# Attention steps traced one at a time between the projections' matmuls, with TensorE held to that order

## The chip, the core and the metric

One core of a Trainium2 chip runs the whole program. The metric is the device time of one execution in microseconds. The engines that matter are TensorE (PE in the rows; its weight loads are listed apart as PEld), VectorE (DVE), ScalarE (ACT) and GpSimd (POOL). They run side by side and wait for one another through semaphores. Matmuls write to PSUM, which has eight banks of 128x512 floats.

## The reference

The program is a two-layer encoder trunk over 256 tokens of width 2048, in float32. Every layer norms its input, projects it, runs attention heads of width 128, multiplies the heads' outputs with a SiLU gate, projects back and adds the residual.

```python
# layer 0
proj = rms_norm(h) @ w_in_even              # q,k,v of A; q,k,v of B; gate
ya = gqa_attention(qa, ka, va)              # 8 heads, q and k normed and rotated
p  = softmax(s1) - lam * softmax(s2)        # 8 differential heads, ALiBi bias
yb = rms_norm(p @ vb, b_subln_g, 1e-5) * (1 - lambda_init)
h  = h + (concat(ya, yb) * silu(gate)) @ w_out_even
# layer 1
yc = 16 heads, softmax(scores + ALiBi + log(window count)) @ vc
h  = h + (yc * silu(gate)) @ w_out_odd
out = rms_norm(h)
```

## The kernel before

**Jobs.** All projections run as jobs. A job (`job_t`, L163) makes 512 output columns for both token tiles (t = 0, 1; 128 tokens each) in two PSUM banks of the pool `acc` (four banks). Its 2048 input channels are 16 steps k. Each float32 product is three single-pass matmuls on float32r halves (`mm3`, L157): high by high, high by low, low by high, at L159, L160 and L161. So a job is 96 matmuls whose weights (the stationary side) are 128 channels by 128 tokens of the activations and whose moving side is 512 columns of the projection matrix. `wgroup` (L135) loads the matrix in pieces of 512 KB, ScalarE rounds each to its high half (L151) and VectorE subtracts to get the low half (L152); both have the planner's high priority. There are 13 jobs of 512 columns for the even input projection, 4 for the even output, 16 for the odd input, and 3 of 512 columns with two of 256 for the odd output.

**Attention.** Results leave a job token-major (tokens on partitions): `evac_t`, `gate_t`, `evac_v` (L212 to L278) scale and copy them. `turned` (L228) transposes a pair of heads, four transposes of 128x128 through TensorE into a bank of the pool `att` (four banks, shared by all of attention). Then each head has six matmuls of 256 columns for its scores (eight for a differential head: four for each of its two softmaxes), a softmax on VectorE and ScalarE, four transposes of the weights p (`transposed`, L312), a split into halves `ph` and `pl`, and the weighted values: six matmuls of 256 columns with v as the stationary side, so the head's output comes out head-major (128 head channels on partitions, 256 tokens along the row), as the output projection wants it.

**A differential head** (`head_b`, L375) needs a norm along the head channels, which lie on partitions. It copies its output out of PSUM (L383), transposes it back to tokens (L388, two), squares and sums, makes the reciprocal root on GpSimd, spreads that over partitions by two more transposes of a broadcast column (L392), and multiplies with the gate, which `pair_gate` (L243) has turned head-major by four transposes for each pair.

**Order.** The program is traced job by job, and whole groups of heads between jobs, but the Tile planner places the instructions. It plays the program on its own timeline and lets each engine take the ready instruction of the highest priority. So TensorE's order is the planner's, and the attention of one group lies among the matmuls of the jobs after it. Each engine then runs its list strictly in that order.

The layer boundary matters too: the output projection of layer 0 (L526) reads `y`, the gated outputs of all 16 heads, and its first job is traced after the last differential head.

Of the kernel before, what the change touches and what calls it, by code (L numbers as in the profile page):

```python
# [17 lines left out]
P = 128  # L18
D = 2048
S = 256  # L20
# [73 lines left out]
def trunk(ctx, tc, x, xt, w_even, w_oe, w_odd, w_oo, gain_cols, rows, final_g, rope_c, geo_c, out):  # L94
# [16 lines left out]
    V, A, G, T = nc.vector, nc.scalar, nc.gpsimd, nc.tensor  # L111
# [45 lines left out]
    def mm3(ps, ah, al, bh, bl, start, stop):  # L157
# [5 lines left out]
    def job_t(w, c0, wd, a, beside=None, pieces=lambda kg: 1):  # L163

        kn = 1024 // wd
        ps = [acc.tile([P, 512], F32, tag="acc", name=f"acc_t{t}")[:, :wd] for t in range(NT)]
        for kg in range(NK // kn):
            hi, lo = wgroup(w, c0, wd, kg, pieces=pieces(kg), beside=beside)
            for t in range(NT):
                for kk in range(kn):  # L170
                    k = kg * kn + kk
                    ts = slice(t * P, (t + 1) * P)
                    mm3(ps[t], a[k][:, 0, ts], a[k][:, 1, ts], hi[:, kk], lo[:, kk], k == 0, k == NK - 1)
        return ps

# [3 lines left out]
    u = [ug[k // UG][:, k % UG] for k in range(NK)]  # L179

    def make_u(k, src, gain):

        A.activation(u[k][:, 0], src, AF.Copy, scale=gain)  # L183
        V.scalar_tensor_tensor(u[k][:, 1], src, gain, f(u[k][:, 0]), op0=ALU.mult, op1=ALU.subtract)
# [43 lines left out]
    def turned(z, pair):  # L228

        ps = att.tile([P, 512], F32, tag="att", name="zt")  # L230
        for j in range(2):
            for t in range(NT):
                c = (2 * pair + j) * HD
                T.transpose(ps[:, j * S + t * P:j * S + (t + 1) * P], z[:, t, c:c + HD], ident)  # L234
        return ps.rearrange("p (j k) -> p j k", j=2)

    def pair_t(z, pair, tag, bufs=2):
        ps = turned(z, pair)
# [4 lines left out]
    def pair_gate(z, pair):  # L243
        ps = turned(z, pair)
        gt = heads.tile([P, 2, S], F32, tag="gate", name="gate", bufs=3)
        A.copy(gt, ps)
        return gt
# [3 lines left out]
    def pair_q64(z, pair):  # L251
        ps = turned(z, pair)
        t = heads.tile([P, 2, 2, S], F32R, tag="q", name="q", bufs=2)
        for j in range(2):
            js, other = slice(64 * j, 64 * j + 64), slice(64 - 64 * j, 128 - 64 * j)
            A.activation(t[js, :, j], ps[js], AF.Copy)
            V.tensor_sub(t[other, :, j], ps[js], f(t[js, :, j]))
        return t

    def pair_k64(z, pair):  # L260
        ps = turned(z, pair)
# [22 lines left out]
    y = [None] * NK  # L284

# [26 lines left out]
    def transposed(p, ps):  # L312
        for kt in range(NT):
            for t in range(NT):
                T.transpose(ps[:, kt * S + t * P:kt * S + (t + 1) * P], p[:, t, kt * P:(kt + 1) * P], ident)  # L315
        ph = heads.tile([P, NT, S], F32R, tag="ph", name="ph")
        pl = heads.tile([P, NT, S], F32R, tag="pl", name="pl")
        pv = ps.rearrange("p (t k) -> p t k", t=NT)
        split(ph, pl, pv)
        return ph, pl  # L320

# [6 lines left out]
    def weighted_v(h, p, v, vs, gate, ps):  # L328
        ph, pl = transposed(p, ps)
        o = ps[:, :S]  # L330
        for kt in range(NT):
            mm3(o, v[:, kt, 0, vs], v[:, kt, 1, vs], ph[:, kt], pl[:, kt], kt == 0, kt == NT - 1)
        finish_y(h, o, gate)

    def head_a(h, q, k, v, vs, gate):
        ps = bank()
        sp = scores(ps, q[:, 0], q[:, 1], k[:, 0], k[:, 1])
# [4 lines left out]
        weighted_v(h, p, v, vs, gate, ps)  # L342
# [13 lines left out]
    def softmax_b(i, q, kh, kl):  # L356
        bias = alibi(2.0 ** -(i + 1), False)
        es, rd = [], []
        for j in range(2):
# [7 lines left out]
            es.append(s)  # L367
        V.tensor_scalar_mul(rd[1], rd[1], nlam[:, 0:1])
# [4 lines left out]
        return p  # L373

    def head_b(h, p, v, vs, gate):  # L375
        ps = [bank(), bank()]
        ph, pl = transposed(p, ps[0])
        o = ps[1][:, :S]
        for kt in range(NT):
# [5 lines left out]
        ot, rb = ps[0][:, :S], ps[0][:, S:]  # L385
        for t in range(NT):
            ts = slice(t * P, (t + 1) * P)
            T.transpose(ot[:, ts], on[:, ts], ident)  # L388
            square_sum(ss[:, t:t + 1], ot[:, ts])
        r = rsqrt_mean(ss, HD, SUBLN_EPS, NT, "rb")  # L390
        for t in range(NT):
            T.transpose(rb[:, t * P:(t + 1) * P], r[:, t:t + 1].to_broadcast([P, P]), ident)  # L392
        V.scalar_tensor_tensor(on, on, gsub[:, 0:1], gate, op0=ALU.mult, op1=ALU.mult)
        finish_y(h, rb, on)

    def softmax_c(h, q, k):
        bias = alibi(float(np.exp2(np.float32(-8.0 * (h + 1) / 16))), True)
        sp = scores(bank(), q[:, 0], q[:, 1], k[:, 0], k[:, 1])
        p = biased(sp, bias)
# [3 lines left out]
        return p  # L403
# [92 lines left out]
    k_a = pair_t(tok_heads(ps_kv, 1, 2), 0, "ka", 1)  # L496
    for g in range(2):
        c = 512 * g
        zq = tok_heads(job_t(w_even, c, 512, u) if g else ps_q0, 0, 4)
        zg = gate_t(job_t(w_even, GATE_E + c, 512, u), rh)  # L500
        for pair in range(2):
            q = pair_t(zq, pair, "q")
            gate = pair_gate(zg, pair)
            for j in range(2):
                head_a(4 * g + 2 * pair + j, q[:, j], k_a[:, g], v_a[:, 0], slice(g * HD, g * HD + HD), gate[:, j])
        zg = gate_t(job_t(w_even, GATE_E + 1024 + c, 512, u), rh)
        zq = evac_t(job_t(w_even, B_Q0 + c, 512, u), rs)
        zk = evac_t(job_t(w_even, B_K0 + c, 512, u), rstd)
        v = v_tile()
        ps = []  # L510
        for pair in range(2):
            q = pair_q64(zq, pair)
            kh, kl = pair_k64(zk, pair)
            ps += [softmax_b(4 * g + 2 * pair + j, q[:, j], kh[:, j], kl[:, j]) for j in range(2)]
        evac_v(v, job_t(w_even, B_V0 + c, 512, u), rstd)
        for pair in range(2):
            gate = pair_gate(zg, pair)
            for j in range(2):
                head_b(8 + 4 * g + 2 * pair + j, ps[2 * pair + j], v[:, pair], slice(j * HD, j * HD + HD), gate[:, j])


    y_even = list(y)
    un = [acts.tile([P, UG, 2, S], F32R, tag="u", name="u", bufs=NK // UG) for _ in range(NK // UG)]
    u = [un[k // UG][:, k % UG] for k in range(NK)]
    parts_o = small.tile([P, NT, 4], F32, tag="parts4", name="parts4", bufs=1)
    for i, (c0, wd) in enumerate(CHUNKS_E):  # L526
        ps = job_t(w_oe, c0, wd, y_even)
        cs = slice(c0, c0 + wd)
        for t in range(NT):
            V.tensor_add(tok[:, t, cs], tok[:, t, cs], ps[t])  # L530
        for k in range(c0 // P, (c0 + wd) // P):
            ps = att.tile([P, 512], F32, tag="att", name="xps")
            for t in range(NT):
                T.transpose(ps[:, t * P:(t + 1) * P], tok[:, t, k * P:(k + 1) * P], ident)
            make_u(k, ps[:, :S], gcol[:, NK + k:NK + k + 1])
        for t in range(NT):
            square_sum(parts_o[:, t, i:i + 1], tok[:, t, cs])


    for g in range(4):  # L540
# [5 lines left out]
        zq = evac_t(job_t(w_odd, c, 512, u), rs)  # L546
        zk = evac_t(job_t(w_odd, D + c, 512, u), rstd)
        p = []
        for pair in range(2):
            q = pair_t(zq, pair, "q")  # L550
            k = pair_t(zk, pair, "k")
            p += [softmax_c(4 * g + 2 * pair + j, q[:, j], k[:, j]) for j in range(2)]
        v = v_tile()
        evac_v(v, job_t(w_odd, 2 * D + c, 512, u), rstd)
        for pair in range(2):
            gate = pair_gate(zg, pair)
            for j in range(2):
                weighted_v(4 * g + 2 * pair + j, p[2 * pair + j], v[:, pair], slice(j * HD, j * HD + HD), gate[:, j], bank())
# [17 lines left out]
    for i, (c0, wd) in enumerate(CHUNKS[:4]):  # L576
        ps = job_t(w_oo, c0, wd, y)
        for t in range(NT):
            final_add(i, t, slice(c0, c0 + wd), ps[t])

    wl = [acts.tile([P, UG, 2, S], F32R, tag="u", name="u", bufs=NK // UG) for _ in range(NK // UG)]
# [58 lines left out]
```

## Time and profile before

| | us |
|---|---|
| median of 3 runs (919.47 to 920.02) | 919.69 |
| the profiled execution | 919.56 |
| its span, first to last instruction | 917.8 |
| TensorE busy | 907.0 |
| VectorE busy | 559.6 |
| ScalarE busy | 532.6 |
| GpSimd busy | 78.2 |

The profiled execution is 0.13 us under the median, and 1.8 us of it lie outside the span. TensorE's granted clock was 0.998 of its full 2.4 GHz over the span. A matmul's recorded time is longer than its share of the engine, because one starts while the one before drains: what an instruction costs TensorE is read from the distance between two starts, not from its own length.

### The profile page before, as it was taken

To read this page: it belongs to the slowest core of one execution; us is meant where nothing else is said; L and a number is where in the kernel's file an instruction comes from. 1 tells how busy PE (TensorE), PEld (TensorE's weight loads), DVE (VectorE), ACT (ScalarE), POOL (GpSimd) and SP (SyncE) were. 2 spreads that over 40 slices of the span, in tenths; PEclk is the share of its full clock that TensorE was granted. 3 is DMA by queue.
4 is the path that set the end of the run, shared out by engine and by line. 5 is a ranking of instruction groups with operands and counts; after the bars stand their busy time and mean duration, and the time that the engine had idled before them with its cause. 6 is when DMAs were issued, how large, how long until landed. Compare 5 with 4: busy or idle time off the path is not lost.

```text
span 917.8 us, 11973 instructions
## 1 busy us (share of the span) xinstructions
PE 907.0 (99%) x4440; PEld 760.4 (83%) x4440; DVE 559.6 (61%) x751; ACT 532.6 (58%) x866; POOL 78.2 (9%) x67
## 2 busy tenths in 40 slices
PE   9999999999999999999999999999999999999996
PEld 7888888888888887888888888888888888888886
DVE  6685644875766686655544765467445754476563
ACT  7657645875576696555544755456544844474451
POOL 0010000110100012000000400032001300040000
PEclk9999999999999999999999999999999999999999
DMA  8855455354544443455555445543554455555552
GB/s 329 311 211 160 154 189 184 138 189 161 179 160 160 171 151 116 169 198 183 184 201 189 154 144 192 196 162 138 186 194 170 147 174 193 193 170 179 194 196 92
DMA packets 47035, 164.39 MB, mean 179 GB/s; under 512 B 5376, under 2 KB 6144, under 8 KB 46976
## 3 DMA queue, kind: packets, MB, share of 16 engines
q1 hardware_dynamic: 46656, 162.57, 50.7%
q0 software_dynamic: 320, 1.05, 0.5%
q8 instruction: 35, 0.57, 0.3%
q14 instruction: 24, 0.20, 0.1%
HBM read 161.50 MB, written 2.10 MB: 178 GB/s over the span
## 4 chain that ended last, share of the span: by engine, by line
PE 96%; ACT 1%; issue 1%; DMA 1%; SPq 0%; DVE 0%; POOLq 0%; POOL 0%; DVEq 0%; ACTq 0%
PE acc_t L160 29%; PE acc_t L161 29%; PE acc_t L159 29%; PE zt L234 2%; PE bank L315 1%; PE bank L159 1%; PE bank L161 1%; PE bank L160 1%; DMA raw<-in_w_in_even 1%; PE bank L294 1%; PE bank L295 1%; PE bank L293 1%; ACT hi L151 0%; PE bank L363 0%; PE bank L364 0%
## 5 line engine op out<-in xcount | busy, mean ns | idle before, releaser
L152 DVE TENSOR_TENSOR lo<-raw,hi 128x1024 fp32r<-128x1024 f32 (+1 forms) x294 | 359.3, 1223 | 284.1 <-ACT hi L151 283.8
L151 ACT ACTIVATE hi<-raw 128x1024 fp32r<-128x1024 f32 (+1 forms) x294 | 309.4, 1054 | 307.7 <-PE acc_t L161 292.0
L160 PE MATMUL acc_t<-lo,u 128*128 128x512 f32 x928 | 364.9, 395 | 0.1
L161 PE MATMUL acc_t<-hi,u 128*128 128x512 f32 x928 | 362.2, 392 | 0.0
L159 PE MATMUL acc_t<-hi,u 128*128 128x512 f32 x928 | 338.4, 393 | 0.4 <-ACT u L183 0.4
L160 PEld LDWEIGHTS acc_t<-lo,u 128*128 128x128 f32 x928 | 174.6, 188 | 36.2 <-DVE lo L152 0.6
L159 PEld LDWEIGHTS acc_t<-hi,u 128*128 128x128 f32 x928 | 174.0, 188 | 36.1 <-ACT u L183 1.2
L161 PEld LDWEIGHTS acc_t<-hi,u 128*128 128x128 f32 x928 | 174.5, 188 | 33.9
L160 PE MATMUL acc_t<-lo,y 128*128 128x512 f32 (+1 forms) x256 | 96.5, 379 | 0.0
L161 PE MATMUL acc_t<-hi,y 128*128 128x512 f32 (+1 forms) x256 | 95.4, 377 | 0.0
L159 PE MATMUL acc_t<-hi,y 128*128 128x512 f32 (+1 forms) x256 | 90.4, 381 | 0.7 <-ACT hi L151 0.6
L351 POOL TENSOR_SCALAR bias<-geo 128x512 f32<-128x512 f32 x24 | 37.5, 1562 | 572.8 <-DVE s L346 534.3
L160 PEld LDWEIGHTS acc_t<-lo,y 128*128 128x128 f32 x256 | 48.3, 189 | 8.6
L159 PEld LDWEIGHTS acc_t<-hi,y 128*128 128x128 f32 x256 | 47.6, 188 | 9.4 <-ACT hi L151 1.4
L161 PEld LDWEIGHTS acc_t<-hi,y 128*128 128x128 f32 x256 | 48.2, 188 | 8.3
L304 ACT ACTIVATE s<-s,nm 128x256 f32<-128x256 f32 x64 | 31.7, 497 | 4.4 <-DVE nm L301 4.3
L216 ACT ACTIVATE z<-acc_t,rstd 128x512 f32<-128x512 f32 x40 | 27.2, 680 | 9.0 <-PE acc_t L161 9.0
L234 PE MATMUL zt<-ident,z 128*128 128x128 f32 x180 | 29.7, 272 | 0.0
L234 PEld LDWEIGHTS zt<-ident,z 128*128 128x128 f32 x180 | 22.4, 140 | 5.0
L346 DVE TENSOR_TENSOR s<-bank,bias 128x512 f32<-128x512 f32 x32 | 21.7, 682 | 6.9 <-POOL bias L353 4.4
L353 POOL TENSOR_TENSOR bias<-bias,geo 128x512 f32<-128x512 f32 x16 | 23.8, 1490 | 1.3
L210 DVE TENSOR_TENSOR pl<-bank,ph 128x512 fp32r<-128x512 f32 x32 | 21.4, 682 | 2.3 <-ACT ph L209 2.2
(137 smaller groups left out, 696.3 us busy)
## 6 DMA issues: line engine op xcount, KB each, us to landing
raw<-in_w_in_odd SPq DMA_DIRECT2D x128, 512.0 KB, 3.2
raw<-in_w_in_even SPq DMA_DIRECT2D x102, 512.0 KB, 3.3
raw<-in_w_out_even SPq DMA_DIRECT2D x32, 512.0 KB, 3.2
raw<-in_w_out_odd SPq DMA_DIRECT2D x32, 512.0 KB, 3.2
tok<-in_x SPq DMA_DIRECT2D x4, 512.0 KB, 8.8
xk<-in_xt SPq DMA_DIRECT2D x6, 256.0 KB, 6.7
raw<-in_w_in_even SPq DMA_DIRECT2D x4, 256.0 KB, 4.0
gf<-in_final_norm_g POOLq DMA_DIRECT2D x4, 256.0 KB, 4.7
```

Source lines behind the costliest of these rows:

```text
L151: A.activation(hi[:, ks], rv[:, ks], AF.Copy)
L152: splits.append(V.tensor_sub(lo[:, ks], rv[:, ks], f(hi[:, ks])))
L159: T.matmul(ps, ah, bh, start=start, stop=False)
L160: T.matmul(ps, ah, bl, start=False, stop=False)
L161: T.matmul(ps, al, bh, start=False, stop=stop)
L210: V.tensor_sub(lo, src, f(hi))
L216: A.activation(z[:, t], ps[t], AF.Copy, scale=r[:, t:t + 1])
L234: T.transpose(ps[:, j * S + t * P:j * S + (t + 1) * P], z[:, t, c:c + HD], ident)
L304: A.activation(e[:, t], s[:, t], AF.Exp, bias=nm[:, t:t + 1], accum_out=den[:, t:t + 1])
L346: V.tensor_add(s, sp, bias)
L351: G.tensor_scalar_mul(b, geo[:, 0], -slope)
L353: G.tensor_add(b, b, geo[:, 1])
```

## The change

The diff has three parts.

1. **One order for TensorE.** A class `T` replaces `nc.tensor`. Each matmul or transpose is traced with `issue_after` the last one, so TensorE runs them exactly as traced.
2. **A tick list.** Attention becomes generators (tasks). `mm3` of a job calls `tick()` after each of its matmuls; a tick runs one step of one due task, and the task names the number of ticks until its next step. A transpose is a step of its own, the six or twelve matmuls of a head are one step. Waiting times are written as ticks: 36, 46 or 40 from scores to the transposes of the weights, 16 from those to the weighted values, 80 from the evacuation of the A queries to their transposes. The output projections (`jobs_out`) interleave their first two jobs: channels of heads 0 to 11 for both, then those of heads 12 to 15 for both.
3. **Token-major differential heads.** The weighted values take `ph` and `pl` as the stationary side and 128 columns of v as the moving side, twelve matmuls in place of six. The output comes out with tokens on partitions, so norm, gain and gate are applied there; two transposes then turn the gated result. The copy at L383, the transposes at L388 and L392 and the gate's transposes for these heads are gone.

```diff
+    class T:
+        last = None
+        @classmethod
+        def queue(cls, op, *args, **kwargs):
+            with tc.issue_after(cls.last) if cls.last else nullcontext():
+                cls.last = op(*args, **kwargs).ins
...
+    def tick():
+        now[0] += 1
+        for task in list(tasks):
+            if task[0] <= now[0]:
+                try:
+                    wait = next(task[1])
...
+                if wait:
+                    task[0] = now[0] + wait
+                    break
...
         T.matmul(ps, ah, bh, start=start, stop=False)
+        tick()
         T.matmul(ps, ah, bl, start=False, stop=False)
+        tick()
         T.matmul(ps, al, bh, start=False, stop=stop)
+        tick()
...
+    def jobs_out(w, chunks, a):
+        (c0, wd), (c1, _) = chunks[:2]
+        ps = [job_banks(wd) for _ in range(2)]
+        for kgs in (range(6), range(6, 8)):
+            for p, c in zip(ps, (c0, c1)):
+                job_steps(p, w, c, wd, a, kgs)
...
     def turned(z, pair):
...
                 T.transpose(ps[:, j * S + t * P:j * S + (t + 1) * P], z[:, t, c:c + HD], ident)
+                yield 1
...
+    def weights_t(p):
+        n = order[0]
+        order[0] += 1
+        yield from until(("parts", n - 2)) if n > 1 else ()
+        ps = bank()
+        for kt in range(NT):
+            for t in range(NT):
+                T.transpose(ps[:, kt * S + t * P:kt * S + (t + 1) * P], p[:, t, kt * P:(kt + 1) * P], ident)
+                yield 1
...
+        split(ph, pl, ps.rearrange("p (t k) -> p t k", t=NT))
+        yield 16
...
-    def head_b(h, p, v, vs, gate):
-        ps = [bank(), bank()]
-        ph, pl = transposed(p, ps[0])
-        o = ps[1][:, :S]
-        for kt in range(NT):
-            mm3(o, v[:, kt, 0, vs], v[:, kt, 1, vs], ph[:, kt], pl[:, kt], kt == 0, kt == NT - 1)
-        on = work.tile([P, S], F32, tag="on", name="on")
-        A.copy(on, o)
...
-            T.transpose(ot[:, ts], on[:, ts], ident)
...
-            T.transpose(rb[:, t * P:(t + 1) * P], r[:, t:t + 1].to_broadcast([P, P]), ident)
...
+        yield 46
+        ph, pl, used = yield from weights_t(p)
+        yield from until(("v", h))
+        v, vs = values[h]
+        zg, gc = gates[h]
+        o = bank()[:, :S]
+        for t in range(NT):
+            for kt in range(NT):
+                ts = slice(t * P, (t + 1) * P)
+                mm3(o[:, ts], ph[:, kt, ts], pl[:, kt, ts], v[:, kt, 0, vs], v[:, kt, 1, vs], t == kt == 0,
+                    t == kt == NT - 1)
...
+            V.scalar_tensor_tensor(yt[:, ts], o[:, ts], r[:, t:t + 1], zg[:, t, gc], op0=ALU.mult, op1=ALU.mult)
+        yield 18
+        ps = bank()[:, :S]
+        for t in range(NT):
+            ts = slice(t * P, (t + 1) * P)
+            T.transpose(ps[:, ts], yt[:, ts], ident)
+            yield 1
...
         zq = tok_heads(job_t(w_even, c, 512, u) if g else ps_q0, 0, 4)
+        spawn(task_a(g, zq), 80)
...
         zk = evac_t(job_t(w_even, B_K0 + c, 512, u), rstd)
+        spawn(task_bk(g, zk, qs), 14)
```

## Rows read from the trace of the kernel before

**Rows 1.** The page: busy time and share of engines, clock, chain that ended last.
```profile
PE 907.0 (99%) x4440; PEld 760.4 (83%) x4440; DVE 559.6 (61%) x751; ACT 532.6 (58%) x866; POOL 78.2 (9%) x67
...
PEclk9999999999999999999999999999999999999999
...
PE 96%; ACT 1%; issue 1%; DMA 1%; SPq 0%; DVE 0%; POOLq 0%; POOL 0%; DVEq 0%; ACTq 0%
```
**Rows 2.** TensorE's groups: line, tiles, shapes, count; busy us, mean ns; idle before.
```profile
L160 PE MATMUL acc_t<-lo,u 128*128 128x512 f32 x928 | 364.9, 395 | 0.1
...
L234 PE MATMUL zt<-ident,z 128*128 128x128 f32 x180 | 29.7, 272 | 0.0
...
L159 PE MATMUL bank<-ph,v 128*128 128x256 f32 x48 | 13.6, 283 | 0.2 <-ACT ph L209 0.2
...
L388 PE MATMUL bank<-ident,on 128*128 128x128 f32 x16 | 4.4, 280 | 0.3 <-ACT on L383 0.3
```
**Rows 3.** TensorE in order of time, 77 to 83 us: start, length, instruction.
```profile
77.32 0.39 PE L159 MATMUL acc_t<-hi,u 128*128 128x512 f32 x1
...
78.68 0.39 PE L160 MATMUL acc_t<-lo,u 128*128 128x512 f32 x1
78.91 0.27 PE L234 MATMUL zt<-ident,z 128*128 128x128 f32 x1
78.94 0.47 PE L161 MATMUL acc_t<-hi,u 128*128 128x512 f32 x1
79.25 0.63 PE L159 MATMUL acc_t<-hi,u 128*128 128x512 f32 x2
...
81.69 0.28 PE L294 MATMUL bank<-ka,q 128*128 128x256 f32 x1
81.81 0.28 PE L295 MATMUL bank<-ka,q 128*128 128x256 f32 x1
81.93 0.60 PE L234 MATMUL zt<-ident,z 128*128 128x128 f32 x4
...
82.60 0.40 PE L160 MATMUL acc_t<-lo,u 128*128 128x512 f32 x1
```
**Rows 4.** TensorE in order of time at the layer boundary, 347 to 350 us.
```profile
347.06 0.60 PE L315 MATMUL bank<-ident,s 128*128 128x128 f32 x4
348.26 0.73 PE L159 MATMUL acc_t<-hi,y 128*128 128x512 f32 x2 [0.59 <-ACT hi L151]
...
349.41 0.28 PE L159 MATMUL bank<-ph,v 128*128 128x256 f32 x1
350.04 0.33 PE L388 MATMUL bank<-ident,on 128*128 128x128 f32 x1 [0.34 <-ACT on L383]
```
**Rows 5.** Busy us and counts of each engine in 340 to 362 us.
```profile
340.00:362.00 22.00, 20.77 (x110) 16.68 (x109) 16.91 (x34) 15.68 (x42) 6.53 (x5) 1.00 0.44 148
```
**Rows 6.** Weight loads (PEld) at 348 us: start, time covered, count.
```profile
348.25 0.30 PEld L159 LDWEIGHTS acc_t<-hi,y 128*128 128x128 f32 x2 [0.83 <-ACT hi L151]
348.60 0.19 PEld L160 LDWEIGHTS bank<-pl,v 128*128 128x128 f32 x1
```
**Rows 7.** A 256-column matmul whose weights could not be loaded ahead.
```profile
355.25 0.38 PE L159 MATMUL bank<-ph,v 128*128 128x256 f32 x1 [0.17 <-ACT ph L209]
```
**Rows 8.** The first score matmul of the first differential head.
```profile
160.47 0.28 PE L363 MATMUL bank<-kh,q 128*128 128x256 f32 x1
```
**Rows 9.** VectorE, the end of the same head's softmax.
```profile
175.07 0.86 DVE L372 SCALAR_TENSOR_TENSOR s<-s,rden 128x256 f32<-128x256 f32 x2
```
**Rows 10.** VectorE, the low half of transposed weights, those of 343.74 us.
```profile
347.57 0.68 DVE L210 TENSOR_TENSOR pl<-bank,ph 128x512 fp32r<-128x512 f32 x1
```
**Rows 11.** TensorE, those four transposes, 343 to 344 us.
```profile
343.74 0.60 PE L315 MATMUL bank<-ident,s 128*128 128x128 f32 x4
```
**Rows 12.** TensorE, the first projection matmuls after the start, two merged.
```profile
5.27 1.20 PE L159 MATMUL acc_t<-hi,u 128*128 128x512 f32 x2
```

**Rows 13.** TensorE, the last matmul.
```profile
909.52 0.28 PE L161 MATMUL acc_l<-u,y 128*128 128x256 f32 x1
```

More of the change, by code (lines that the diff above doesn't have):

```diff
@@ L155, in wgroup, with spawn, until, advance @@
         return hi, lo
-    def mm3(ps, ah, al, bh, bl, start, stop):
+    tasks, now, done = [], [0], set()
+    def spawn(steps, delay=1):
+        tasks.append([now[0] + delay, steps])
+    def tick():
[4 more added lines that the diff above has]
+                    wait = next(task[1])
+                except StopIteration:
+                    tasks.remove(task)
+                    wait = 1
+                if wait:
+                    task[0] = now[0] + wait
+                    break
+    def until(key):
+        while key not in done:
+            yield 0
+    def advance(finished):
+        while not finished():
+            assert tasks
+            now[0] += 1
+            for task in list(tasks):
+                if task[0] <= now[0]:
+                    try:
+                        task[0] = now[0] + next(task[1])
+                    except StopIteration:
+                        tasks.remove(task)
+    def mm3(ps, ah, al, bh, bl, start, stop, tick=lambda: None):
         T.matmul(ps, ah, bh, start=start, stop=False)
+        tick()
         T.matmul(ps, ah, bl, start=False, stop=False)
+        tick()
         T.matmul(ps, al, bh, start=False, stop=stop)
-    def job_t(w, c0, wd, a, beside=None, pieces=lambda kg: 1):
+        tick()
+    def job_banks(wd):
+        return [acc.tile([P, 512], F32, tag="acc", name=f"acc_t{t}")[:, :wd] for t in range(NT)]
+    def job_steps(ps, w, c0, wd, a, kgs, beside=None, pieces=lambda kg: 1):
         kn = 1024 // wd
-        ps = [acc.tile([P, 512], F32, tag="acc", name=f"acc_t{t}")[:, :wd] for t in range(NT)]
-        for kg in range(NK // kn):
+        for kg in kgs:
             hi, lo = wgroup(w, c0, wd, kg, pieces=pieces(kg), beside=beside)
@@ L241, in pair_t, with pair_gates @@
         return dst
[L243 to L247, printed above, removed]
+    def pair_gates(z, key):
+        for pair in range(2):
+            ps = yield from turned(z, pair)
+            gt = heads.tile([P, 2, S], F32, tag="gate", name="gate", bufs=3)
+            A.copy(gt, ps)
+            for j in range(2):
+                gates[key + 2 * pair + j] = gt[:, j]
+                done.add(("gate", key + 2 * pair + j))
     def pair_q64(z, pair):
-        ps = turned(z, pair)
+        ps = yield from turned(z, pair)
         t = heads.tile([P, 2, 2, S], F32R, tag="q", name="q", bufs=2)
@@ L260, in pair_k64 @@
     def pair_k64(z, pair):
-        ps = turned(z, pair)
+        ps = yield from turned(z, pair)
         kh = heads.tile([P, 2, 2, S], F32R, tag="k", name="kh", bufs=2)
@@ L284, in trunk @@
     y = [None] * NK
+    gates, values, order = {}, {}, [0]
     def bank():
@@ L326, in finish_y, with weighted_v, head_a @@
         split(y[h][:, 0], y[h][:, 1], yf)
-    def weighted_v(h, p, v, vs, gate, ps):
-        ph, pl = transposed(p, ps)
-        o = ps[:, :S]
+    def weights_t(p):
[7 more added lines that the diff above has]
+                yield 1
+        ph = heads.tile([P, NT, S], F32R, tag="ph", name="ph")
+        pl = heads.tile([P, NT, S], F32R, tag="pl", name="pl")
+        split(ph, pl, ps.rearrange("p (t k) -> p t k", t=NT))
+        yield 16
+        return ph, pl, ("parts", n)
+    def weighted_v(h, p, key):
+        ph, pl, used = yield from weights_t(p)
+        yield from until(("v", key))
+        v, vs = values[key]
+        o = bank()[:, :S]
         for kt in range(NT):
             mm3(o, v[:, kt, 0, vs], v[:, kt, 1, vs], ph[:, kt], pl[:, kt], kt == 0, kt == NT - 1)
[L333 to L337, printed above, removed]
+        done.add(used)
+        yield from until(("gate", h))
+        finish_y(h, o, gates[h])
+    def head_a(h, q, k):
+        sp = scores(bank(), q[:, 0], q[:, 1], k[:, 0], k[:, 1])
         p = stile()
@@ L341, in head_a @@
             A.activation(p[:, t], p[:, t], AF.Copy, scale=rden[:, t:t + 1])
-        weighted_v(h, p, v, vs, gate, ps)
+        yield 36
+        yield from weighted_v(h, p, h)
     def biased(sp, bias):
@@ L402, in softmax_c, with set_values @@
             A.activation(p[:, t], p[:, t], AF.Copy, scale=rden[:, t:t + 1])
-        return p
+        yield 40
+        yield from weighted_v(h, p, h)
+    def set_values(v, h, n=4):
+        for i in range(n):
+            values[h + i] = (v[:, i // 2], slice(i % 2 * HD, i % 2 * HD + HD))
+            done.add(("v", h + i))
     parts = small.tile([P, NT, 4], F32, tag="parts", name="parts", bufs=1)
@@ L495, in trunk, with task_ka, task_a, task_bq @@
     evac_v(v_a, ps_kv, rstd, 256)
-    k_a = pair_t(tok_heads(ps_kv, 1, 2), 0, "ka", 1)
+    keys_a = []
+    def task_ka(z):
+        keys_a.append((yield from pair_t(z, 0, "ka", 1)))
+    def task_a(g, zq):
+        for pair in range(2):
+            q = yield from pair_t(zq, pair, "q")
+            yield 16
+            for j in range(2):
+                h = 4 * g + 2 * pair + j
+                values[h] = (v_a[:, 0], slice(g * HD, g * HD + HD))
+                done.add(("v", h))
+                spawn(head_a(h, q[:, j], keys_a[0][:, g]), 1 + 20 * j)
+            yield 22
+    def task_bq(zq, qs):
+        for pair in range(2):
+            qs.append((yield from pair_q64(zq, pair)))
+    def task_bk(g, zk, qs):
+        for pair in range(2):
+            h = 8 + 4 * g + 2 * pair
+            kh, kl = yield from pair_k64(zk, pair)
+            yield 20
+            for j in range(2):
+                spawn(head_b(h + j, h + j - 8, qs[pair][:, j], kh[:, j], kl[:, j]), 1 + 24 * j)
+            yield 26
+            yield from until(("scores", h + 1))
+    spawn(task_ka(tok_heads(ps_kv, 1, 2)), 50)
     for g in range(2):
@@ L499, in trunk @@
         zq = tok_heads(job_t(w_even, c, 512, u) if g else ps_q0, 0, 4)
+        spawn(task_a(g, zq), 80)
         zg = gate_t(job_t(w_even, GATE_E + c, 512, u), rh)
[L501 to L505, printed above, removed]
+        spawn(pair_gates(zg, 4 * g), 22)
         zg = gate_t(job_t(w_even, GATE_E + 1024 + c, 512, u), rh)
-        zq = evac_t(job_t(w_even, B_Q0 + c, 512, u), rs)
+        for i in range(4):
+            gates[8 + 4 * g + i] = zg, slice(i * HD, i * HD + HD)
@@ L508, in trunk @@
+        zq, qs = evac_t(job_t(w_even, B_Q0 + c, 512, u), rs), []
+        spawn(task_bq(zq, qs), 14)
         zk = evac_t(job_t(w_even, B_K0 + c, 512, u), rstd)
+        spawn(task_bk(g, zk, qs), 14)
         v = v_tile()
[L510 to L514, printed above, removed]
-        evac_v(v, job_t(w_even, B_V0 + c, 512, u), rstd)
@@ new lines, in trunk, with task_u @@
+        set_values(v, 8 + 4 * g)
+    ug = [acts.tile([P, UG, 2, S], F32R, tag="u", name="u", bufs=NK // UG) for _ in range(NK // UG)]
+    parts_o = small.tile([P, NT, 4], F32, tag="parts4", name="parts4", bufs=1)
+    u = [None] * NK
+    def task_u(cs):
+        for k in range(cs.start // P, cs.stop // P):
+            ps = bank()[:, :S]
+            for t in range(NT):
+                T.transpose(ps[:, t * P:(t + 1) * P], tok[:, t, k * P:(k + 1) * P], ident)
+                yield 1
+            make_u(k, ps, gcol[:, NK + k:NK + k + 1])
@@ L529, in trunk @@
+    for i, cs, ps in jobs_out(w_oe, CHUNKS_E, y):
         for t in range(NT):
             V.tensor_add(tok[:, t, cs], tok[:, t, cs], ps[t])
[L531 to L535, printed above, removed]
+        spawn(task_u(cs), 8)
         for t in range(NT):
@@ L537, in trunk, with task_q, task_k @@
             square_sum(parts_o[:, t, i:i + 1], tok[:, t, cs])
+    y = [None] * NK
+    gates.clear()
+    values.clear()
+    done.clear()
+    done.update(("parts", n) for n in range(order[0]))
+    def task_q(zq, qs):
+        for pair in range(2):
+            qs.append((yield from pair_t(zq, pair, "q")))
+    def task_k(g, zk, qs):
+        for pair in range(2):
+            h = 4 * g + 2 * pair
+            k = yield from pair_t(zk, pair, "k")
+            yield 16
+            for j in range(2):
+                spawn(head_c(h + j, qs[pair][:, j], k[:, j]), 1 + 16 * j)
+            yield 12
@@ L545, in trunk @@
         zg = gate_t(ps, rh)
-        zq = evac_t(job_t(w_odd, c, 512, u), rs)
+        spawn(pair_gates(zg, 4 * g), 22)
+        zq, qs = evac_t(job_t(w_odd, c, 512, u), rs), []
+        spawn(task_q(zq, qs), 14)
         zk = evac_t(job_t(w_odd, D + c, 512, u), rstd)
[L548 to L552, printed above, removed]
+        spawn(task_k(g, zk, qs), 14)
         v = v_tile()
         evac_v(v, job_t(w_odd, 2 * D + c, 512, u), rstd)
[L555 to L558, printed above, removed]
+        set_values(v, 4 * g)
     parts = small.tile([P, NT, 5], F32, tag="parts5", name="parts5", bufs=1)
@@ L574, in final_add @@
             V.tensor_mul(z, z, gfs(cs))
-    for i, (c0, wd) in enumerate(CHUNKS[:4]):
-        ps = job_t(w_oo, c0, wd, y)
+    for i, cs, ps in jobs_out(w_oo, CHUNKS[:4], y):
         for t in range(NT):
-            final_add(i, t, slice(c0, c0 + wd), ps[t])
+            final_add(i, t, cs, ps[t])
+    advance(lambda: not tasks)
     wl = [acts.tile([P, UG, 2, S], F32R, tag="u", name="u", bufs=NK // UG) for _ in range(NK // UG)]
```

62 lines of the change are left out of this document (31 added, 31 removed).

## The prediction

> **What bounds the kernel now.** I read the page first. TensorE is busy for 907.0 of 917.8 us, VectorE and ScalarE for about 60% each, the clock is at its upper level throughout, and 96% of the chain that ended last is TensorE [rows 1]. So the time is the sum of what TensorE's instructions cost, plus a start, a tail and whatever stalls remain. The tail after the last matmul is not touched.
>
> Second, the prices. They come from distances between starts, since the lengths of some 0.39 us [rows 2] contain the drain. Six projection matmuls from 77.32 to 78.68 us give 0.2267 us for 512 columns; two 256-column matmuls start 0.12 us apart [rows 3]. A transpose next to another costs 0.11: from the 256-column matmul at 81.81 to the projection matmul at 82.60 lie 0.79 us, less 0.12 and 0.227, for four transposes [rows 3]. One transpose alone between projection matmuls costs 0.116 to 0.12: 78.68 to 79.25 is 0.57, less twice 0.227 [rows 3]; there are 29 of these. It is not cheaper alone, it is about 0.008 dearer.
>
> Third, the sum. 3,456 projection matmuls of 512 columns at 0.2267 are 783.5 us, 592 of 256 columns (192 in the last jobs, 400 in attention) at 0.12 are 71.0, 372 transposes at 0.11 are 40.9: 895.4. From the first projection matmul at 5.27 us [rows 12] to the last, at 909.5 [rows 13], TensorE has 904 us. Only some 9 us are neither. Where are they? Subtracting prices from starts all along the trace: 2.1 us in the first 20 us, while the first loads arrive; 2.5 us between 347 and 361 us [rows 4, 5]; 0.3 us at 383 us; the rest a few nanoseconds at a time, rounding included. The attention in all other stretches is already packed without a stall. This limits what any new order can bring.
>
> **Part 1, the stalls at the layer boundary.** When the first output job starts, the last differential heads are still in work, TensorE has only that job left, and each step waits for ScalarE. After four transposes at 347.06 (0.44 us) a matmul starts at 348.26, 0.8 us late; the transpose at 350.04 is 0.5 late after the matmul at 349.41 [rows 4]. Six such stalls come to 2.5 us; in this stretch the busy time is 1.2 us short of 22.00 even with the drains counted in [rows 5]. With `jobs_out` the channels of heads 12 to 15 are needed only after 144 projection matmuls, 33 us, and a head has about 100 ticks of its own steps and waits (46, 16 and 18 among them). I take these off, with the one at 383 us: **-2.8 us**. What is late next there is nothing I can see: the two banks of the second job are free once v is evacuated, 72 matmuls earlier than they are needed.
>
> **Part 2, one transpose for each tick.** The 340 transposes that are left each stand alone: 340 x 0.008 = 2.7 us, less what about 90 groups pay now, 0.7: **+2.0 us**. That the bursts are broken up gives nothing back by these prices: six matmuls in a row cost what six single ones do.
>
> **Part 3, the differential heads.** Each loses two transposes of its output and two of the broadcast column (16 of the first kind [rows 2], as many of the second) and its share of the gate's, two (16 of the 180 [rows 2]), and gains two: 32 fewer, x 0.11 = **-3.5 us**. The copies and squares that go lie on ScalarE beside TensorE: nothing, as long as no tick count runs out (below).
>
> Its six 256-column matmuls (48 for eight heads; the 48 of L159 are one line of three for 24 heads [rows 2]) become twelve of 128 columns. No single-pass matmul of this width is in the trace. Bounds: a line through 0.2267 and 0.12 gives 0.067 at 128 columns [rows 3]; as dear as the widest would be 0.227. Which one? It also needs its weights. Two rows show what a load costs when it can't run ahead: two loads cover 0.30 us where one takes 0.19, so the second began 0.11 after the first [rows 6], and a 256-column matmul behind a wait is 0.10 longer than its like, 0.38 against 0.28 [rows 7]. So a load of 128 float32r columns occupies its path for 0.11 us; a 256-column matmul just covers that, one of 128 columns can't. I take 0.11, the load: 96 x 0.11 - 48 x 0.12 = 10.6 - 5.8 = **+4.8 us** (bounds +0.7 and +16.0).
>
> The Trainium skill (TensorE: Matmul & The Clock Gate, Back-to-back issue gap) has a stream of load and matmul at 128 columns sustain some 81 ns each. By it this term would be +2.0 us, an estimate, and the whole 2.8 us less. The loads of this trace at 0.11 speak against it, so I keep it for a rival.
>
> **Part 4, the order itself.** TensorE now waits wherever a step comes before its data; what stands behind is every later matmul, since nothing may pass. A tick is at least 0.227 us. From a head's transposed weights to its weighted values there are 16 ticks, 3.6 us; the slowest such split in the trace ends at 348.25, 4.1 us after transposes that are through at 344.18 [rows 10, 11]. The low half is first needed by the second or third matmul. If that slowest case came at a few of the 32 heads, 0.2 to 0.5 each, it would be between 0 and 1.5 us; I take **+0.8 us**. At the very start the planner put two high-by-high matmuls ahead of the first low half [rows 12]; in the fixed order one of them waits, at most 0.2, inside that bound. No DMA is moved past another except that the first two output jobs' loads alternate; SP's queue runs ahead by four buffers in both.
>
> **The sum.** Against the profiled 919.56: -2.8 + 2.0 - 3.5 + 4.8 + 0.8 = +1.3, 920.8; the median stands 0.13 above that execution: **920.9 us**.
>
> **Rivals.**
>
> *Narrow matmuls are cheap.* Loads hide after all, in the 0.067 of the line: the term is +0.7 and the time 916.8; half hidden, at 0.09, it would be 919.0. For it: the recorded lengths of neighbouring loads overlap, 0.30 us for two of 0.19 [rows 6]. Against: their starts stay 0.11 apart. (The skill's figure above would make this rival 918.1, an estimate.)
>
> *Narrow matmuls are dear.* Single-pass float32r at 128 columns pays a full-width price, 0.227: 932.1 us. For it: no row excludes it, and all of the kernel's such matmuls have 256 columns or more. Against: 256 and 512 columns lie on one line that leaves only 0.013 at zero columns [rows 3].
>
> *The ticks are too short.* Place: a differential head's softmax. It is given 4 + 4 + 46 ticks from its first score matmul, 12.2 us; in the trace the first such head's took from 160.47 to 175.93, 15.5 us, with two heads at once in VectorE's queue and nobody in need of it [rows 8, 9]. If that is its real length beside the splits, TensorE stops 3.3 us; the two heads of a pair overlap, so four times: +13, 933.9 us. It decides from the point where a softmax takes over 12.2 us. Against: heads now start 24 ticks apart, and steps within a tick lengthen it to about 0.25 us.
>
> *The boundary stalls stay* (the interleaving doesn't do what it says, for instance because the second job's banks are late): 2.8 back, 923.7.
>
> **How the numbers follow.** A measurement can tell about 0.2%, 1.84 us, from no change: below 917.9 counts as faster, above 921.5 as slower. My forecast has 0.57, and its own range, 918.5 to 923.0, crosses the upper limit: 0.02 faster, 0.35 the same, 0.20 slower. Cheap narrow matmuls 0.16: 0.12 faster, 0.04 the same. Dear ones 0.13, slower. Too few ticks 0.10, slower. Boundary stalls 0.04, 0.02 of it within the limit with the other terms low. In all 0.14 faster, 0.41 the same, 0.45 slower. For 8 in 10 the range takes in most of the cheap case and about half of the two dear ones: 916.5 to 932.5.
>
> **What would show it.** In the new profile, the starts of a head's twelve 128-column matmuls: 0.11 apart if I am right, 0.07 or 0.23 for the rivals. TensorE's instruction count: 4,440 - 32 + 48 = 4,456. Single transposes between projection matmuls with 0.57 us across the two. Between the layers no TensorE wait over 0.3 us. Waits of TensorE for ScalarE or VectorE ahead of the transposes of p would show the ticks too short. The forecast is wrong if the narrow matmuls are not near 0.11, or if new waits of TensorE add up to more than 2 us.

## The result, and the profile after

The changed kernel takes 954.65 us (953.89 to 957.42 in 4 runs) where the kernel before took 919.63 beside it: 1.0386 times as long, with a 95% interval of 1.0364 to 1.0407. That is 35.0 us slower. I had forecast 920.9 with a range up to 932.5.

The page of the profiled execution (955.2 us), lines as in [rows 1]:

```profile
span 953.3 us, 11973 instructions
...
PE 925.4 (97%) x4456; PEld 765.5 (80%) x4456; DVE 566.9 (59%) x751; ACT 532.4 (56%) x854; POOL 84.7 (9%) x67
...
PEclk9999999999999999999999899999999899999998
...
PE 87%; ACT 5%; DVE 2%; POOL 2%; issue 2%; DMA 1%; SPq 0%; POOLq 0%; DVEq 0%; ACTq 0%
```

TensorE has 4,456 instructions, as counted ahead. But TensorE's share of the chain that ended last has gone from 96% to 87%: TensorE now waits. For whom, by the view of waits, TensorE alone (waiting tile, who ended the wait: total, times, longest):

```profile
PE bank L120 <- DVE v L357: 6.5, 8, 0.9
PE bank L120 <- ACT kl L348: 5.8, 2, 2.9
PE bank L120 <- ACT v L356: 5.0, 4, 1.3
PE bank L120 <- DVE yt L485: 1.4, 1, 1.4
```

Three places, then. The weighted values wait for v to be evacuated (L356, L357), in each of the four groups of layer 1. Score matmuls of differential heads wait for the low half of k (L348), twice. A transpose waits for a gated output once (L485). The drains hide a part of such a wait in this view; from start to start the 15 come to some 23 us. Here is one place of the first kind, TensorE in order of time:

```profile
534.81 0.63 PE L120 MATMUL acc_t<-hi,u 128*128 128x512 f32 x2
535.47 0.38 PE L120 MATMUL bank<-ph,v 128*128 128x256 f32 x1
535.69 0.28 PE L120 MATMUL bank<-pl,v 128*128 128x256 f32 x1
536.81 0.38 PE L120 MATMUL bank<-ph,v 128*128 128x256 f32 x1 [0.85 <-DVE v L357]
538.45 0.54 PE L120 MATMUL bank<-ph,v 128*128 128x256 f32 x1 [1.25 <-ACT v L356]
538.78 0.42 PE L120 MATMUL bank<-pl,v 128*128 128x256 f32 x1
539.80 0.58 PE L120 MATMUL bank<-ph,v 128*128 128x256 f32 x1 [0.59 <-DVE v L357]
540.18 0.63 PE L120 MATMUL acc_t<-lo,u 128*128 128x512 f32 x1
540.60 1.05 PE L120 MATMUL acc_t<-hi,u 128*128 128x512 f32 x2
...
541.88 1.05 PE L120 MATMUL acc_t<-hi,u 128*128 128x512 f32 x2
542.74 0.63 PE L120 MATMUL acc_t<-lo,u 128*128 128x512 f32 x1
543.16 1.05 PE L120 MATMUL acc_t<-hi,u 128*128 128x512 f32 x2
```

Six matmuls that cost 0.7 us take from 535.47 to 540.18. The reader is to see two things. First, one head's matmuls meet v half by half: each row with a bracket is the next half of v arriving. Second, what comes after: from 540.60 to 541.88 there are three projection matmuls, 0.427 us each, where 0.227 is the price [rows 3]. The clock has halved. Busy time in stretches (after the comma TensorE's busy us and count; the third number from the end is the granted clock):

```profile
520.00:534.00 14.00, 14.00 (x76) 11.72 (x75) 9.28 (x14) 9.11 (x22) 8.73 (x6) 1.00 0.35 117
534.00:540.00 6.00, 3.28 (x14) 1.96 (x13) 5.35 (x8) 5.20 (x11) 2.92 (x2) 0.88 0.47 169
540.00:546.00 6.00, 6.00 (x19) 4.60 (x19) 0.85 (x2) 1.09 (x2) 0.00 (x0) 0.55 0.24 87
546.00:552.00 6.00, 6.00 (x36) 5.12 (x35) 4.07 (x6) 2.94 (x5) 0.00 (x0) 1.00 0.26 89
```

TensorE was busy all the way from 540 to 546 us and still got through 19 instructions where the next 6 us hold 36 (some of these are shorter ones). ScalarE, in order of time, shows why v was so late:

```profile
534.75 0.67 ACT L356 ACTIVATE v<-acc_t,rstd 128x512 fp32r<-128x512 f32 x1
535.32 0.50 ACT L384 ACTIVATE s<-s,nm 128x256 f32<-128x256 f32 x1
...
536.30 0.57 ACT L284 ACTIVATE ph<-bank 128x512 fp32r<-128x512 f32 x1
536.78 1.04 ACT L168 ACTIVATE hi<-raw 128x1024 fp32r<-128x1024 f32 x1
537.73 0.67 ACT L356 ACTIVATE v<-acc_t,rstd 128x512 fp32r<-128x512 f32 x1
```

The two evacuations of v, 0.67 us each, stand 3 us apart: the planner, which still orders ScalarE, put one head's softmax (L384), the split of another's weights (L284) and a weight half (L168) between them. Nothing on ScalarE knows that all of TensorE stands behind the second one.

A place of the second kind, TensorE in order of time, and under it two stretches (columns as above). The second of these two score matmuls waits for the low half of k, and the clock falls behind it:

```profile
176.72 0.28 PE L120 MATMUL bank<-kh,q 128*128 128x256 f32 x1
179.88 0.39 PE L120 MATMUL bank<-kl,q 128*128 128x256 f32 x1 [2.88 <-ACT kl L348]
```

```profile
174.00:180.00 6.00, 3.12 (x18) 2.37 (x18) 5.09 (x10) 5.86 (x11) 0.00 (x0) 1.00 0.25 87
180.00:186.00 6.00, 6.00 (x27) 5.12 (x28) 4.12 (x9) 3.87 (x12) 1.49 (x1) 0.72 0.28 90
```

Subtracting the prices of the prediction from the starts, place by place, shows where the time went: the four groups of layer 1 lose 25.0 us (some 15 waiting, the rest the clock), the two waits for k 9.5 us (6.1 waiting), the gated output 1.6 us, the start 0.25 us (the 96th projection matmul starts at 29.15 instead of 28.89 us). The stalls between the layers are gone, -2.7. The two profiled executions are 35.6 us apart, so some 1.9 us of that are left for the instructions themselves. By their prices (+2.0 - 3.5 + 4.8) these should cost 3.3 more; where the difference went is not shown.

### The profile page after: what moved, and what is told of

The parts are those of the page before. It is cut to its first block, busy times and chain, and to the rows that moved or that the text cites. A ratio compares the mean times of both kernels' runs of the same rounds, so it can differ in the third digit from the quotient of the medians.

```text
span 953.3 us, 11973 instructions
## 1 busy us (share of the span) xinstructions
PE 925.4 (97%) x4456; PEld 765.5 (80%) x4456; DVE 566.9 (59%) x751; ACT 532.4 (56%) x854; POOL 84.7 (9%) x67
## 4 chain that ended last, share of the span: by engine, by line
PE 87%; ACT 5%; DVE 2%; POOL 2%; issue 2%; DMA 1%; SPq 0%; POOLq 0%; DVEq 0%; ACTq 0%
PE acc_t L120 78%; PE bank L120 7%; ACT hi L168 2%; PE zt L120 2%; POOL bias L441 1%; POOL bias L443 1%; DVE lo L169 1%; ACT s L384 1%; PE acc_l L120 1%; DMA raw<-in_w_in_even 1%; DVE s L436 1%; ACT v L356 0%; ACT s L503 0%; DVE v L357 0%; ACT ph L284 0%
## 5 line engine op out<-in xcount | busy, mean ns | idle before, releaser
L120 PE MATMUL acc_t<-hi,u 128*128 128x512 f32 x1856 | 603.1, 403 | 0.2 <-ACT u L258 0.2
L168 ACT ACTIVATE hi<-raw 128x1024 fp32r<-128x1024 f32 (+1 forms) x294 | 309.6, 1053 | 317.5 <-PE acc_t L120 301.0
L120 PE MATMUL acc_t<-lo,u 128*128 128x512 f32 x928 | 373.9, 403 | 0.1
L120 PE MATMUL acc_t<-hi,y 128*128 128x512 f32 (+1 forms) x512 | 157.2, 388 | 0.0
L441 POOL TENSOR_SCALAR bias<-geo 128x512 f32<-128x512 f32 x24 | 43.0, 1790 | 605.5 <-DVE s L436 579.6
L120 PE MATMUL zt<-ident,z 128*128 128x128 f32 x164 | 44.4, 271 | 0.0
L120 PE MATMUL bank<-ident,s 128*128 128x128 f32 x128 | 35.3, 276 | 0.0
L384 ACT ACTIVATE s<-s,nm 128x256 f32<-128x256 f32 x64 | 31.8, 498 | 1.1 <-DVE nm L381 1.0
L120 PE MATMUL bank<-ph,v 128*128 128x256 f32 x64 | 17.2, 316 | 11.6 <-DVE v L357 6.5
L120 PEld LDWEIGHTS bank<-ph,v 128*128 128x128 f32 x64 | 11.5, 192 | 16.2 <-DVE v L357 8.2
L284 ACT ACTIVATE y<-yf 128x256 fp32r<-128x256 f32 x24 | 9.9, 413 | 22.3 <-DVE yf L394 22.3
```

Source lines behind the costliest of these rows:

```text
L120: cls.last = op(*args, **kwargs).ins
L168: A.activation(hi[:, ks], rv[:, ks], AF.Copy)
L284: A.activation(hi, src, AF.Copy)
L384: A.activation(e[:, t], s[:, t], AF.Exp, bias=nm[:, t:t + 1], accum_out=den[:, t:t + 1])
L441: G.tensor_scalar_mul(b, geo[:, 0], -slope)
```

## Experiments

Theory W: the loss is TensorE waiting in its fixed order where the tick counts allow too little, plus the clock behind such waits. Theory I: the new steps themselves (single transposes, narrow matmuls) cost more than their prices, and the waits only take up slack.

**Later v.** Only the moment changes at which the waiting heads are told that v is there:

```diff
-        set_values(v, 4 * g)
+        spawn(late_values(v, 4 * g), 8)
```

`late_values` calls `set_values`, here 8 ticks later. Layer 0 has the same edit, and a second kernel has 24 ticks in both.

> The changed kernel, with v declared ready to the waiting heads 8 ticks after the v job instead of at its end (8 groups of heads; nothing else moves). Theory W (the loss is TensorE waiting in its fixed order for data that its tick counts do not allow for, and the clock that halves after such a wait): of the 3.6 us that TensorE waits in each of the four layer-1 groups for v's evacuation about 1.8 us are left, too short for the clock to fall, so 4 x (1.8 + 2.5) = 17 us come back: 937 to 940. Theory I (single transposes and narrow matmuls cost more than their price everywhere, the waits are cover for that): under 4 us come back, 950 to 955.

Measured 941.81 us (ratio 1.0247, 1.0230 to 1.0264).

> As the one before with 24 ticks, 5.5 us, which is more than the evacuation of v takes. Theory W: no wait for v is left in layer 1 and the clock stays up there: 954.7 - 25 = 930. Theory I: as for 8 ticks, 950 to 955.

Measured 930.78 us (ratio 1.0119, 1.0104 to 1.0135): 23.9 us back, as theory W has it. With 24 ticks the profile has no wait for v left. With 8 it has two waits of about 1.0 us in each group, and the clock behind them is not the same each time (columns as above):

```profile
535.00:541.00 6.00, 4.30 (x25) 3.31 (x24) 4.15 (x7) 4.52 (x10) 1.14 (x1) 1.00 0.48 175
638.00:644.00 6.00, 5.36 (x22) 4.52 (x23) 3.62 (x7) 2.45 (x5) 0.00 (x0) 0.72 0.38 126
840.00:846.00 6.00, 5.87 (x24) 4.89 (x25) 3.50 (x7) 2.49 (x4) 0.55 (x1) 0.72 0.45 115
```

So my "too short for the clock to fall" held in two of four groups. In the other two the slow clock cost about 1.5 us each, which is most of the 2 to 5 us by which this run missed.

**Later scores too.** Adds `yield 40` for `yield 20` ahead of the differential heads' scores.

> v after 24 ticks, and 40 in place of 20 ticks between the transposes of the differential heads' keys and their scores. Theory W: the two waits of 3.0 us for the low half of k go too, with about 2 us of slow clock behind each: 930 - 10 = 920, what is left over the kernel before being the start (2.3 us), one wait of 1.5 us for a gated output, and the narrow matmuls, less the boundary's stalls. Theory I: still above 945.

Measured 922.93 us (ratio 1.0034, 1.0021 to 1.0047), 7.9 back where 10 were expected. The waits for k are gone, but 40 more ticks for a group made the last heads' y late: two new waits of 0.8 and 0.7 us for it.

**Waits filled with work.** Sixteen matmuls whose result nobody uses, at the end of each v job of layer 1, split the wait from the clock:

```diff
+        spare = bank()
+        for i in range(16):
+            T.matmul(spare, ug[0][:, 0, 0, :P], ug[0][:, 1].rearrange("p a b -> p (a b)"), start=True, stop=True)
         set_values(v, 4 * g)
```

> The changed kernel with 16 extra matmuls of 512 columns (3.6 us, their result is not used) at the end of each of the four v jobs of layer 1, where TensorE otherwise waits as long for v. So the wait is filled with work of the same length and nothing else is taken away. If a part of the loss is the clock that halves behind the wait: that part, 2.2 to 3.3 us a group by the profile, goes away although TensorE does more: 954.7 - 11 = 944. If the time behind the waits is late weight halves or a backlog on ScalarE and VectorE: no change, 953 to 957.

Measured 947.64 us (ratio 1.0296, 1.0280 to 1.0312). TensorE did 64 matmuls more, 14.5 us of work, and the program ended 7.0 us earlier. TensorE of this kernel in order of time:

```profile
536.52 3.79 PE L120 MATMUL bank<-u 128*128 128x512 f32 x16
540.15 0.39 PE L120 MATMUL acc_t<-hi,u 128*128 128x512 f32 x1
540.38 0.28 PE L120 MATMUL bank<-ph,v 128*128 128x256 f32 x1
```

Its busy time and clock in the same stretch:

```profile
534.00:540.00 6.00, 6.00 (x30) 4.91 (x29) 5.61 (x10) 5.55 (x12) 2.95 (x2) 1.00 0.49 161
540.00:546.00 6.00, 5.85 (x34) 4.84 (x33) 2.63 (x5) 2.64 (x5) 0.00 (x0) 1.00 0.29 101
```

The clock stays at 1.00 and 34 instructions go through in 540 to 546. So in layer 1 the waits cost their 15 us and the clock behind them some 8 to 10 more. I expected 944; 0.3 us of wait was left in each group, and behind the second wait for k, which this edit does not touch, the clock stayed low for longer than in the first profile, which cost 1.3 us more.

**The planner's order.** The class `T` calls the operation without `issue_after`; trace order, ticks, interleaved output jobs and token-major heads stay.

```diff
-            with tc.issue_after(cls.last) if cls.last else nullcontext():
-                cls.last = op(*args, **kwargs).ins
+            op(*args, **kwargs)
```

> The changed kernel with its trace order, ticks and token-major heads, but TensorE free to be ordered by the planner (no issue_after). Theory W: the planner moves each step behind its data, so the waits go: 916 to 921. Theory I: the single transposes and narrow matmuls are all still there, so 945 or more.

Measured 918.98 us (ratio 0.9991, 0.9981 to 1.0000), and 918.83 (0.9989, 0.9980 to 0.9998) when it ran again:

> The same kernel as planner_order once more, on the chip and beside the runs of planner_mixed: 918.5 to 919.5.

This is the run that decides between the theories: TensorE runs the same 4,456 instructions and 35.7 us are gone. The loss is the fixed order. One reservation: the planner puts most single transposes together again (some 50 of the 340 stay alone between two projection matmuls), which by the prices is worth 2 us, not 35.

**Can the fixed order be mended?** Two attempts, with v after 24 ticks, 33 ticks before the scores and the first 96 projection matmuls free; the second also has 24 ticks for 16 between the weights' transposes and the weighted values:

> The fixed order with three ticks mended: v ready after 24 ticks, 33 ticks instead of 20 between the differential keys and their scores, and the first 96 projection matmuls (the start) left to the planner. By theory W all waits but a wait at the gated output and parts of the start are gone. Against 922.9 with 40 ticks: -1.6 for the wait at the last heads' y, which the longer ticks had pushed behind the matmuls that need it, and -2 for the start: 919.0 to 919.8, that is the price of the narrow matmuls and single transposes less the layer boundary's stalls, with nothing gained over the kernel before.

Measured 925.67 us (ratio 1.0064, 1.0051 to 1.0076): a miss of 6.

> As fixed_order_mended, with 24 ticks in place of 16 between the transposes of the weights and the weighted values, for all heads. The two waits of 1.6 us for the low half of the weights and the slow clock behind the first go: 925.7 - 5 = 920.5 to 921, unless the longer ticks push the last heads' y behind the matmuls that need it (then 922 to 923). A time below 919 would mean that the fixed order can gain something by itself.

Measured 925.03 us (ratio 1.0056, 1.0043 to 1.0069): a miss of 4, and of 2 against the 922 to 923 that it names for a late y. TensorE's waits in the first attempt:

```profile
PE bank L122 <- DVE pl L287: 3.0, 2, 1.5
PE acc_t L122 <- ACT u L260: 1.2, 2, 0.7
...
PE bank L122 <- DVE yt L487: 0.5, 1, 0.5
```

And in the second:

```profile
PE bank L122 <- DVE yt L487: 2.6, 2, 1.3
PE bank L122 <- ACT kl L350: 2.1, 2, 1.1
```

Each tick that was lengthened moved every later step against the other engines' queues, and another wait came up: the low half of the weights, then the gated output and k again. The freed start brought nothing that can be seen; there was only 0.25 us in it, and my 2 us in the expectation were a miscount.

**Token-major heads alone,** in the kernel before, its planner's order and trace as they were (new body of `head_b`, no gate transposes):

> The kernel before, planner's order and trace as they were, with the token-major differential heads alone. By the prices: 32 transposes fewer, -3.5 us, and 96 matmuls of 128 columns for 48 of 256, +4.8 to +5.1: 920.9 to 921.3. If the shorter chain of the last heads shortens the stalls between the layers as well, up to 1.5 less: 919.5. A price of 0.067 for a narrow matmul would give 916.9, one of 0.227 would give 932.

Measured 923.65 us (ratio 1.0044, 1.0031 to 1.0056), 4.1 us slower. **Interleaved output jobs alone,** in the kernel before:

> The kernel before with the first two jobs of the even output projection interleaved (channels of heads 0 to 11 for both, then the rest), nothing else. If the stalls between the layers come from a lack of other matmuls while the last heads finish, 2.5 us go: 917.2. If they come from the planner's order itself, within 0.5 of 919.7.

Measured 921.54 us (ratio 1.0024, 1.0014 to 1.0034), 2.0 us slower: both expectations missed, and the reason I had given for the boundary's stalls with them. **Head-major again** in the planner's order of the new trace (part 3 undone):

> The trace order with ticks, TensorE left to the planner, and the differential heads' weighted values and norm head-major again as in the kernel before (part 3 undone). By the prices the token-major form costs 1.3 us on TensorE: 919.0 - 1.3 = 917.7. If token-major is free or a gain in this order, 919.0 or more; if it costs what it cost alone in the planner's old trace order (4.1 us), 914.9.

Measured 921.10 us (ratio 1.0015, 1.0006 to 1.0025): the 917.7 by the prices missed too, and the case "free or a gain in this order", 919.0 or more, came. The three have the place in common. The stretch from 340 to 400 us follows for five kernels, to be read by TensorE's busy time out of 60 us (columns as above). The kernel before:

```profile
340.00:400.00 60.00, 58.67 (x290) 47.79 (x289) 39.78 (x66) 36.01 (x80) 7.92 (x7) 1.00 0.46 159
```

Token-major alone:

```profile
340.00:400.00 60.00, 56.52 (x283) 45.86 (x282) 37.90 (x65) 33.48 (x74) 7.47 (x7) 1.00 0.46 155
```

Interleaved output jobs alone:

```profile
340.00:400.00 60.00, 56.78 (x282) 46.33 (x281) 39.53 (x66) 35.45 (x78) 8.66 (x7) 1.00 0.46 152
```

Head-major in the planner's order of the new trace:

```profile
340.00:400.00 60.00, 57.37 (x287) 46.99 (x286) 40.56 (x64) 35.13 (x77) 8.05 (x7) 1.00 0.46 154
```

The planner's order of the whole change:

```profile
340.00:400.00 60.00, 59.81 (x311) 50.20 (x310) 41.32 (x65) 35.33 (x73) 8.78 (x7) 1.00 0.49 164
```

Each of the two parts alone makes TensorE idle more at the layer boundary, not less, and so does the new trace without the short token-major chain; the trace spread over ticks, the interleaving and the short chain together make it busy throughout. Why the planner packs this stretch worse with a part of the three missing is not settled: it places the last heads by its own estimates, and each kernel may get another order there.

**Mixed.** If the boundary is where the short chain pays and the price counts elsewhere, only the last four differential heads should be token-major:

```diff
+        if h < 12:
+            ...head-major as in the kernel before
+            return
```

> Trace order with ticks, TensorE left to the planner; the first four differential heads head-major as in the kernel before, the last four (those that finish at the layer boundary) token-major. By the prices the four head-major heads save half of 1.3 us, and the boundary keeps the short chain: 919.0 - 0.65 = 918.3. If what brought the boundary's stalls back in planner_head_major was the head-major form anywhere, 920 to 921.

Measured 918.29 us (ratio 0.9983, 0.9974 to 0.9992), on the forecast, 0.54 below planner_order beside it, and the lowest median of all. It is 1.5 us, 0.17%, below the kernel before. That the prices made the 0.54 is not shown: the runs of the two kernels overlap (917.87 to 918.88, 918.29 to 919.07), and in the three runs before this one the planner's new order moved the time by 2 to 3.5 us against the forecasts.

## Why the prediction was wrong

**The bound and the prices** held. A single transpose costs 0.118 us in the changed kernel. TensorE in order of time: with one transpose ahead of each, these two projection matmuls are three steps apart, 0.344 us each, which is 0.227 and 0.117:

```profile
62.50 0.48 PE L120 MATMUL acc_t<-hi,u 128*128 128x512 f32 x1
...
63.53 0.70 PE L120 MATMUL acc_t<-hi,u 128*128 128x512 f32 x2
```

The twelve narrow matmuls of a head, the term with the widest bounds, cost 0.11 each. TensorE in order of time, one head:

```profile
184.44 0.33 PE L120 MATMUL bank<-v,ph 128*128 128x128 f32 x2
184.61 0.27 PE L120 MATMUL bank<-v,pl 128*128 128x128 f32 x1
184.72 0.38 PE L120 MATMUL bank<-v,ph 128*128 128x128 f32 x2
184.94 0.28 PE L120 MATMUL bank<-v,pl 128*128 128x128 f32 x1
...
185.61 0.28 PE L120 MATMUL bank<-v,pl 128*128 128x128 f32 x1
185.73 0.45 PE L120 MATMUL acc_t<-hi,u 128*128 128x512 f32 x1
```

From the row at 184.61 to that at 184.94 are three of them: 0.33 us. The whole burst of twelve adds 1.353 us (from the projection matmul at 184.21 to the second one behind it, at 186.02, less two of 0.227), 0.113 each. So the reading of exposed weight loads [rows 6, 7] was right. The rivals of cheap and of dear narrow matmuls both fall.

The Trainium skill (TensorE: Matmul & The Clock Gate, Back-to-back issue gap) has 81 ns for such a stream. This trace does not agree, 113 ns for these float32r matmuls, and the measurement decides.

**Part 1, the boundary: -2.8.** Right in the sum (-2.7), wrong in its reason: interleaving alone did not remove the stalls of [rows 4, 5]. That the sum came out is in part luck.

**Parts 2 and 3: +2.0, -3.5, +4.8.** The prices were right (0.113 makes the last term +5.1); the sum is less sure, since the changed kernel has 1.9 us for these terms where they make 3.3. In the planner's order, without part 4, and without the 2.0 us for single transposes, most of which the planner puts together again, the terms give -1.5; the whole change measured -0.7 and -1.0. Half of part 3 undone moved 0.54 us where 0.65 were expected, but part 3 alone cost 4.1 where the prices give 1.3.

**Part 4, the order itself: +0.8.** This is the step that failed; its term was about 36 us. I said that TensorE waits wherever a step comes before its data, and then looked at two chains only, from the weights' transposes to their halves [rows 10, 11] and through the softmax [rows 8, 9]. (The first of these was also misread by a little: the slowest split in the trace is not the one that ends at 348.25 but those of layer 1, 4.3 us, one of them up to 527.97. No wait came of it.) I did not go through every `until`. The one that asks for v is satisfied in the trace the moment the evacuation is traced, with no tick after it: the weighted values are put right behind the v job, although two passes of ScalarE and two of VectorE lie between. And the scores of a differential head's second softmax need six ScalarE passes on k (L345, L346 and L348, each twice). The 20 ticks between k's transposes and the scores, 4.5 us, and the few behind them cover these only while ScalarE's queue holds little else: ahead of the sixth pass it ran two evacuations of v, a weight half and the split of another head's weights, from 176.48 to 179.18 us.

The rival *the ticks are too short* named the right mechanism at the wrong place (the softmax chains, which turned out fast enough) and for 13 us. It was too small on two counts: the waits themselves came to some 23 us, and behind them the clock cost another 12 or 13, over a third of the loss, where the rival priced a wait at its length.

## What to carry to other kernels

When a change fixes the order of the engine that bounds the kernel, list every wait that the new order can meet, one by one, and ask for each which queue its releaser stands in; a gap counted in another engine's instructions holds only as long as that queue is short. A wait of the bounding engine is not priced at its length: look at the granted clock behind it, in more than one execution, since equal waits did not cost the same. And before taking an order from a planner, see what the planner's order loses: here it was 3 us in 918, so there was little to win and each missed wait to pay.

## What the runs showed of the hardware

The granted clock went from its 2.4 GHz level to 1.2 GHz behind waits of TensorE of 3.0 us (the scores at 176.72, then 179.88) and behind some 3.7 to 4.0 us of waits broken by single matmuls (layer 1); it stayed up behind one wait of 1.5 us (the gated output at 217.5).

The length of a wait alone does not tell. Behind two waits of 1.0 us close to one another the clock fell in two groups of four (8 ticks for v). And with 24 ticks for v, where both waits of 3.0 us for k are still there, it stayed at 1.00 behind the first (177 to 183 us) and was 0.76 behind the second (340 to 346 us). Why is not shown.

The Trainium skill (TensorE: Matmul & The Clock Gate, HAM oscillation — how this bites in real kernels) describes a kernel whose waits put TensorE back to its slow clock again and again, so that they cost more than their length. This trace agrees: at most 14 us of the 35 by the mean granted clock, 0.983 over 953.3 us against 0.998; at most, because TensorE waited through a part of the slow stretches.

I had read that the clock was at its upper level throughout [rows 1] and not asked what kept it there.
